# Neighbourhood-attention layer on one core: q and k of 14 heads computed first, as seven half-block products, through DRAM

## The chip, the core and the metric

The kernel runs on one core of a Trainium2 chip. The core has TensorE (PE, with its weight loads shown apart as PEld), VectorE (DVE), ScalarE (ACT), GpSimd (POOL) and SyncE (SP), which only starts transfers here; POOL starts transfers too. Each engine runs its instructions in the order in which they were written and waits for the others through semaphores. The metric is the time of one execution on the device, in microseconds (us).

## The reference, cut to what matters

All data is float32; the model width is 2048, there are 512 latent tokens (8 rows of 64), 256 context tokens and 16 heads of 128.

```python
h  = modulate(x,   sh1,  sc1)                  # 512 x 2048
hc = modulate(ctx, csh1, csc1)                 # 256 x 2048
q, k, v  = split(h @ w_qkv)                    # 16 heads of 128
k_c, v_c = split(hc @ w_qkv[:, 2048:])         # the context gives k and v alone
s_win = q_blk . k_blk * scale + bias           # 4 column bands of 128 queries; a band sees 2 or 3 key blocks of 128
s_ctx = q_blk . k_c * scale
p = softmax(concat([s_win, s_ctx]))            # one softmax over 256 or 384 window keys and 256 context keys
y = (p_win @ v_blk + p_ctx @ v_c) @ w_o
x = layer_norm(alpha * x + g1 * y)
x = layer_norm(alpha * x + g2 * swiglu(modulate(x, sh2, sc2)))
```

The shifts, scales and gates come from `silu(c) @ ada_w` (and from `c_ctx` for hc).

## The kernel before, in words

Each float32 operand of a large product is held as two parts, hi and lo, and each product is three matmuls (`mm3`): hi*hi, hi*lo, lo*hi. Weights come as raw tiles of 128x1024 (512 KB) on SP's queue; `pieces` (through `split`, L77 and L78) makes hi on ACT and lo on DVE. All matmuls are written by L81.

1. **Start phase.** For each of 16 slices of the width, `ada_start` streams four raw tiles `wr_an` through PE to get the modulation, `h_start` modulates a slice of x and of ctx and splits them into `a_h` and `hc`, and `qkv_start` accumulates q, k, v of heads 0 and 1 in seven banks `acc` (raw tiles `wr_w`). At its end the banks are split straight into the tiles that attention reads.
2. **Seven periods, one for each further pair of heads** (`hp` = 1 to 7). `v_block` makes v of both heads for the 6 token blocks (288 matmuls of 256 columns, banks `vp`). Then for each head `q_block` (48 matmuls of 512 columns, banks `qp`) and `k_block` (48 of 512 columns, `kp`, and 48 of 256 columns for the context, `cp`). Between them stand `ada_tile`s: two raw tiles `wr_ada` and two DVE multiply-and-sum instructions each (L141), which give the shifts, scales and gates that later stages need; 9 in each period, 64 in all.
3. **Attention.** `attn` cuts a head into 11 steps: four `score(j)` (matmuls into `sc` and `sl`, two maxima and a negation on DVE, two exponentials on ACT, the sum, its reciprocal and the scaling of p, L305, on DVE), then seven steps that transpose p, split it into `th` and `tl` and multiply by v into `o`. `enqueue` puts the steps in a list and `pop`, called between groups of matmuls, takes one now and then: head 2hp beside `k_block` of the next head (16 places), head 2hp+1 beside the next `v_block` (24 places). The result `ob` of a head goes to `oT` in DRAM on POOL's queue. DVE, ACT and POOL run what is written in that same order.
4. **Output projection** (`o_load`, `wo_half`), with attention of the last head beside it, and the remaining output blocks, LayerNorm, the feed-forward part and its LayerNorm. These products are `Pair`s run by `run`: a 2x2 arrangement of half blocks computed with seven half products in place of eight (24 matmuls of 256 columns each), with sums of weight halves on DVE (L623) and results put together from three banks (`post`).

A pool's tiles come free when their last reader is done, and a new pool that takes the place of an old one waits for all that used the old. `rp[0]` names the pool of raw tiles: `p0` with 6 buffers in the start phase, `p1r` with 3 in the periods. The lines that the change and the steps of the prediction touch: L77, L78, L141, L208 (load of x), L295 to L305 (softmax), L318 (transposes), L343 (`oT` write).

```python
            turn["mm"] = 0
            enqueue(attn(0, q0, k0, v0), 16)
            v_block(0, v0, [4, 5])
            for hp in range(1, NH // 2):
                if hp == 1:
                    enqueue(attn(1, q1, k1, v0), 24)
                v = new_v(hp)
                v_block(hp, v, list(range(6)))
                flush()
```

Of the kernel before, what the change touches and what calls it, by code (L numbers as in the profile page):

```python
# [17 lines left out]
P = 128  # L18
# [19 lines left out]
RAWBUFS = {"wraw": None, "r11": 2, "r22": 2, "r21": 1, "r12": 1}  # L38

# [4 lines left out]
def build(tc, ins, out):  # L44
    nc = tc.nc
    with ExitStack() as top:
# [60 lines left out]

        cv = base.tile([P, 2, KT], F32, name="cv")
# [43 lines left out]
        hcx = [cu_tile(k, F32R, f"hc{k}") for k in range(KT // 2)]  # L152
        hc_hi = [hcx[k // 2][:, k % 2 * T:k % 2 * T + C] for k in range(KT)]
        hc_lo = [hcx[k // 2][:, k % 2 * T + C:k % 2 * T + T] for k in range(KT)]

        with ExitStack() as ph1:
            pa = ph1.enter_context(tc.tile_pool(name="pa", bufs=1))

            def stage(name):
                return pa.tile([P, T], F32, tag="stg", name=name, bufs=2)  # L160

            def new_q(h):
                return [pa.tile([P, T], F32R, tag=f"q{i}", name=f"q{h}_{i}", bufs=2) for i in "hl"]

            def new_k(h):
                return [pa.tile([P, T + C], F32R, tag=f"k{i}", name=f"k{h}_{i}", bufs=2) for i in "hl"]

            def new_v(hp):
                return [[pa.tile([P, 2 * P], F32R, tag=f"v{t}{i}", name=f"v{hp}_{t}{i}") for i in "hl"]
                        for t in range(6)]  # L170

            def evac_q(ps, q):
                nc.scalar.activation(q[0], ps, AF.Copy, scale=QSCALE)
                nc.vector.scalar_tensor_tensor(out=q[1], in0=ps, scalar=QSCALE, in1=q[0].bitcast(F32),
                                               op0=ALU.mult, op1=ALU.subtract)

            q0, q1, k0, k1, v0 = new_q(0), new_q(1), new_k(0), new_k(1), new_v(0)
# [3 lines left out]

            accs = [bank(i, f"acc{i}") for i in range(7)]
            rows, mods = {}, {}
# [21 lines left out]
            def h_start(kt):  # L205
                md = mods.pop(kt)
                xr = stage(f"xr{kt}")
# [4 lines left out]
                cr = stage(f"cr{kt}")  # L212
                nc.gpsimd.dma_start(cr[:, :C], ins["ctxT"][kt])
# [4 lines left out]
            def qkv_start(kt):  # L218
                wh, wl = unit(ins["w0"][kt], f"w0{kt}", 768)
                f, l = kt == 0, kt == KT - 1  # L220
                for i in range(4):
                    sl = slice(i * P, (i + 1) * P)
                    mm3(accs[i], wh[:, sl], wl[:, sl], act_hi[kt], act_lo[kt], f, l)
                if kt + 1 < KT:
                    ada_cols(kt + 1)
# [940 lines left out]
```

## Time and profile before

| | us |
|---|---|
| median of 3 runs | 2516.32 |
| lowest and highest run | 2513.05, 2521.82 |
| the profiled execution, its own time | 2523.26 |
| its span in the trace | 2521.5 |
| busy in the span: PE, DVE, ACT, POOL | 2431.2, 1836.2, 1039.7, 232.1 |

Busy time is the time in which an engine runs instructions other than register, branch, semaphore and transfer-starting ones, so a busy PE can still be one whose matmuls follow each other more slowly than they could. The profiled execution lies 6.9 us above the median, and the sum below is made against it: from the span's start to 155.4 us is the start phase, from there to 945.3 us lie the first attention, the periods and the beginning of the output projection, whose first matmul starts there.

### The profile page before, as it was taken

To read this page: it belongs to the slowest core of one execution; us is meant where nothing else is said; L and a number is where in the kernel's file an instruction comes from. 1 tells how busy PE (TensorE), PEld (TensorE's weight loads), DVE (VectorE), ACT (ScalarE), POOL (GpSimd) and SP (SyncE) were. 2 spreads that over 40 slices of the span, in tenths; PEclk is the share of its full clock that TensorE was granted. 3 is DMA by queue.
4 is the path that set the end of the run, shared out by engine and by line. 5 is a ranking of instruction groups with operands and counts; after the bars stand their busy time and mean duration, and the time that the engine had idled before them with its cause. 6 is when DMAs were issued, how large, how long until landed. Compare 5 with 4: busy or idle time off the path is not lost.

```text
span 2521.5 us, 45143 instructions
## 1 busy us (share of the span) xinstructions
PE 2431.2 (96%) x18588; PEld 2303.4 (91%) x18588; DVE 1836.2 (73%) x2619; ACT 1039.7 (41%) x1590; POOL 232.1 (9%) x348
## 2 busy tenths in 40 slices
PE   7999999999999999999999999999999989999997
PEld 5688989888898988999999999999999989999996
DVE  2365655566565568899888888878888877878877
ACT  2242322222232235548444444444444544545555
POOL 1110100000010000110110100101001000000020
PEclk9999999999999999999999999999999999999998
DMA  8874444454455463745443434434344565755684
GB/s 328 317 246 151 153 162 134 153 163 151 155 156 163 128 202 130 191 100 187 136 136 118 136 124 138 137 120 133 125 144 156 182 186 134 210 146 134 175 185 118
DMA packets 142543, 406.18 MB, mean 161 GB/s; under 512 B 16544, under 2 KB 40496, under 8 KB 142208
## 3 DMA queue, kind: packets, MB, share of 16 engines
q1 hardware_dynamic: 116608, 342.42, 41.2%
q0 software_dynamic: 25728, 60.88, 9.9%
q8 instruction: 145, 2.38, 0.4%
q14 instruction: 62, 0.51, 0.1%
HBM read 351.85 MB, written 40.89 MB: 156 GB/s over the span
## 4 chain that ended last, share of the span: by engine, by line
issue 38%; PE 34%; DMA 11%; DVE 9%; POOL 4%; ACT 2%; SPq 0%; POOLq 0%; DVEq 0%; ACTq 0%
DMA wr_ada<-ada_t 7%; PE qp L81 6%; PE kp L81 4%; PE vp L81 3%; PE cp L81 2%; PE g_1b L81 2%; POOL setT L594 2%; DVE wr_ada L141 2%; PE y L81 2%; PE g_3b L81 1%; PE g_5b L81 1%; PE g_4b L81 1%; PE g_2b L81 1%; PE g_0b L81 1%; POOL setB L594 1%
## 5 line engine op out<-in xcount | busy, mean ns | idle before, releaser
L623 DVE TENSOR_TENSOR wr_f<-wr_f,wr_f 128x1024 f32<-128x1024 f32 x164 | 199.7, 1218 | 3.1 <-DMA wr_f<-w_in 1.7
L81 PE MATMUL vp<-wh_v,a_h 128*128 128x256 f32 x896 | 167.7, 279 | 0.0
L141 DVE CUSTOM_DVE_ANT_0 wr_ada<-wr_ada,s_c,bin 128x1024 f32<-128x1024 f32 x64 | 84.2, 1316 | 89.2 <-DMA wr_ada<-ada_t 88.9
L81 PEld LDWEIGHTS vp<-wh_v,a_h 128*128 128x128 f32 x896 | 141.2, 188 | 0.6
L81 PE MATMUL kp<-a_h,wh_k 128*128 128x512 f32 x448 | 141.2, 396 | 0.0
L81 PE MATMUL qp<-a_h,wh_q 128*128 128x512 f32 x448 | 140.6, 395 | 0.0
L141 DVE CUSTOM_DVE_ANT_0 wr_ada<-wr_ada,s_c,adap 128x1024 f32<-128x1024 f32 x64 | 82.2, 1284 | 79.3 <-DMA wr_ada<-ada_t 79.1
L81 PE MATMUL vp<-wl_v,a_h 128*128 128x256 f32 x448 | 125.1, 279 | 0.0
L623 DVE TENSOR_TENSOR wr_g<-wr_g,wr_g 128x896 f32<-128x896 f32 (+1 forms) x96 | 107.6, 1130 | 6.5 <-DMA wr_g<-w_out 5.5
L77 ACT CAST th<-tr 128x256 fp32r<-128x256 f32 (+2 forms) x96 | 45.8, 477 | 155.0 <-PE tr L318 154.9
L81 PEld LDWEIGHTS cp<-hc,wh_k 128*128 128x128 f32 x448 | 84.1, 188 | 20.3
L594 POOL DMA_DIRECT2D setB<-h x66 | 35.6, 542 | 711.1 <-DVE h L1008 692.6
L81 PE MATMUL vp<-wh_v,hc 128*128 128x256 f32 x512 | 98.3, 280 | 0.0
L81 PEld LDWEIGHTS qp<-a_h,wh_q 128*128 128x128 f32 x448 | 82.0, 188 | 16.5
L81 PE MATMUL cp<-hc,wh_k 128*128 128x256 f32 x448 | 89.5, 281 | 0.0
L301 ACT ACTIVATE p<-sc,sm 128x256 f32<-128x256 f32 x64 | 30.4, 475 | 143.2 <-DVE sm L299 143.2
L81 PE MATMUL qp<-a_h,wl_q 128*128 128x512 f32 x224 | 88.6, 395 | 0.0
L81 PE MATMUL kp<-a_h,wl_k 128*128 128x512 f32 x224 | 88.4, 395 | 0.0
L78 DVE TENSOR_TENSOR tl<-tr,th 128x256 fp32r<-128x256 f32 (+2 forms) x96 | 52.4, 552 | 48.0 <-ACT th L77 48.0
L81 PEld LDWEIGHTS vp<-wl_v,a_h 128*128 128x128 f32 x448 | 84.2, 188 | 0.6
L81 PEld LDWEIGHTS vp<-wh_v,hc 128*128 128x128 f32 x512 | 81.6, 188 | 0.1
L274 POOL TENSOR_TENSOR bv<-br,mask 128x256 f32<-128x256 f32 (+1 forms) x48 | 43.3, 928 | 399.9 <-DVE sm L304 370.3
(1882 smaller groups left out, 8516.1 us busy)
## 6 DMA issues: line engine op xcount, KB each, us to landing
wr_f<-w_in SPq DMA_DIRECT2D x164, 512.0 KB, 4.1
wr_ada<-ada_t SPq DMA_DIRECT2D x128, 512.0 KB, 3.9
wr_an<-ada_n SPq DMA_DIRECT2D x64, 512.0 KB, 7.4
wr_g<-w_out SPq DMA_DIRECT2D x64, 448.0 KB, 4.5
wr_v<-w_v SPq DMA_DIRECT2D x32, 512.0 KB, 4.6
wr_g<-w_out SPq DMA_DIRECT2D x32, 512.0 KB, 4.3
wr_q<-w_qk SPq DMA_DIRECT2D x28, 512.0 KB, 4.6
wr_k<-w_qk SPq DMA_DIRECT2D x28, 512.0 KB, 3.7
```

What stands on the lines that cost most here:

```text
L77: nc.scalar.copy(hi, src)
L78: nc.vector.tensor_tensor(out=lo, in0=src, in1=hi.bitcast(F32), op=ALU.subtract)
L81: nc.tensor.matmul(ps, a, b, start=start, stop=stop, skip_group_check=True)
L141: nc.vector.tensor_tensor_reduce(out=raw, in0=raw, in1=s_c[:, half * U:(half + 1) * U], scale=1.0, scalar=bin2[:, i:i + 1] if half == 0 el ...
L274: nc.gpsimd.tensor_tensor(out=bv[:, off:off + n * P].rearrange("p (d r k) -> p d r k", d=n, r=8), in0=brv[:, d0:d0 + n], in1=mask[:, off:o ...
L301: nc.scalar.activation(p[:, nl:nl + C], sc[:, :C], AF.Exp, bias=sm[:, 2:3], accum_out=sm[:, 3:4])
L594: nc.gpsimd.dma_start(setD[n][q], src)
L623: nc.vector.tensor_tensor(out=self.r[out][:, :n], in0=self.r[a][:, :n], in1=self.r[b][:, :n], op=op)
```

## The change

- **Start phase.** The slices come in the order 0, 8, 1, 9, ... The split `hc` tiles go to DRAM (`hcD`, 16 writes of 256 KB on POOL's queue). `h_sums` builds, from the x tiles of slices k and k+8, the four sums of activation halves that the seven half products need (`T1` to `T4`: 4 sums and 4 splits of 256 columns for each of 8 pairs of slices). At the end the seven banks `acc` are copied (ACT and DVE in turn) to tiles `st` and written to DRAM (`qkD`, `v0D`, `kc0D`).
- **A new stage** of 14 `QKPair`s (q and k of seven head pairs; 168 matmuls of 256 columns each), whose results go to `qkD` in DRAM. Beside them 14 `ada_tile`s.
- **Then** `hc` is loaded back (8 loads of 512 KB on SP's queue), and `v_block(0)` runs alone. A period is now `v_block` with attention of *both* heads of the pair before (22 steps at 24 places) and 7 ada tiles, then for each head a load of q and k from `qkD` (`qk_load`, POOL's queue, through the two `stg` buffers) and the context half of `k_block`. Attention of the last two heads, not of one, stands beside the output projection.
- **p is scaled on ACT**, not on DVE.
- `Pair` and `run` are moved up unchanged, but for the pool of their result tiles.

```diff
                     nc.vector.reciprocal(sm[:, 6:7], sm[:, 5:6])
-                    nc.vector.tensor_scalar_mul(p, p, sm[:, 6:7])
+                    nc.scalar.activation(p, p, AF.Identity, scale=sm[:, 6:7])
                     st[j] = (p, nl)
...
+                hcs[kt] = pa.tile([P, 2, C], F32R, tag="hcs", name=f"hcs{kt}", bufs=2)
+                split(hcs[kt][:, 0], hcs[kt][:, 1], cr)
+                nc.gpsimd.dma_start(hcD[kt], hcs[kt].bitcast(F32))
...
+            def h_sums(kk):
+                a, b = xs.pop(kk), xs.pop(kk + 8)
+                z = (a[:, HA], a[:, HB], b[:, HA], b[:, HB])
+                for n, d, x, y, op in (("T3", 1, 3, 1, ALU.subtract), ("T2", 0, 1, 0, ALU.add),
+                                       ("T4", 2, 2, 0, ALU.subtract), ("T1", 3, 3, 0, ALU.subtract)):
+                    nc.vector.tensor_tensor(out=z[d], in0=z[x], in1=z[y], op=op)
+                    split(sets[n](kk, 0), sets[n](kk, 1), z[d])
...
+                for i, dst in enumerate((qkD[0][0], qkD[1][0], qkD[0][1], qkD[1][1], v0D[0], v0D[1], kc0D)):
+                    st = p0.tile([P, T], F32, tag="xs", name=f"st{i}", bufs=4)
+                    if i % 2:
+                        nc.vector.tensor_copy(st, accs[i])
+                    else:
+                        nc.scalar.copy(st, accs[i])
+                    nc.gpsimd.dma_start(dst, st)
+            class QKPair(Pair):
...
+                    elif p == "P2":
+                        ada_more(1)
...
+            with tc.tile_pool(name="p1x", bufs=2) as p1x:
+                rp[0] = p1x
+                ev[0] = p1x
...
+                run([QKPair(w, j) for j in range(1, NH // 2) for w in range(2)], {})
...
+                    ada_more((2, 2, 2, 1)[u] if len(tl) > 2 else 0)
+                flush()
...
-            def q_block(h, q):
...
+            def qk_load(h):
+                q, k = new_q(h), new_k(h)
+                for w in range(2):
+                    st = stage(f"qk{w}_{h}")
+                    nc.gpsimd.dma_start(st, qkD[w][h])
...
-                        mm3(kb, hi[:, s_], lo[:, s_], act_hi[kt], act_lo[kt], kt == 0, kt == KT - 1)
                         mm3(cb[:, :C], hi[:, s_], lo[:, s_], hc_hi[kt], hc_lo[kt], kt == 0, kt == KT - 1)
...
             for hp in range(1, NH // 2):
-                if hp == 1:
-                    enqueue(attn(1, q1, k1, v0), 24)
+                enqueue(attn(2 * hp - 2, *qk[0], v) + attn(2 * hp - 1, *qk[1], v), 24)
                 v = new_v(hp)
                 v_block(hp, v, list(range(6)))
-                flush()
-                ada_more(3)
-                for i in range(2):
-                    h = hp * 2 + i
-                    q, k = new_q(h), new_k(h)
-                    q_block(h, q)
-                    ada_more(1)
-                    k_block(h, k)
-                    ada_more(2)
-                    flush()
-                    enqueue(attn(h, q, k, v), 16 if i == 0 else 24)
+                qk = []
+                for h in (2 * hp, 2 * hp + 1):
+                    qk.append(qk_load(h))
+                    k_block(h, qk[-1][1])
...
-            rate[0] = 12 / 21
+            enqueue(attn(NH - 2, *qk[0], v) + attn(NH - 1, *qk[1], v), 21)
```

Three places show how the instructions now stand. First, SP's queue where the start phase ends: `wr_w07` and `wr_w015` are the last weights of the start phase, `wr_v0_...` those of the first v block, `wr_qk0_1_...` those of the first new pair, and a row's brackets name the semaphores for which it waits. Before:

```order
81 L105 DMA wr_w015_1339<-w0 128x768 [waits DMAHW2_49,DVE_49]
82 L105 DMA wr_v0_0_1408<-w_v 128x1024
83 L105 DMA wr_v0_1_1462<-w_v 128x1024
84 L105 DMA wr_v0_2_1510<-w_v 128x1024 [waits DMAHW3_49]
```

Changed:

```order
80 L110 DMA wr_w07_1393<-w0 128x768 [waits DMAHW1_49,PE_49]
81 L110 DMA wr_w015_1445<-w0 128x768 [waits DMAHW2_49,DVE_49]
82 L153 DMA wr_qk0_1_11_1520<-w_qk 128x1024 [waits DMASW6_49,DMASW5_49,DMASW7_49,DMASW4_49,DMAHW0_49,DMASW3_49,DMAHW3_49,DMASW2_49,DMAHW4_49,DMASW1_49,DMAHW5_49,DMASW0_49,DMAHW6_49,DVE_49,DMAHW7_49,Activation_49,Pool_49]
83 L153 DMA wr_qk0_1_22_1522<-w_qk 128x1024
84 L153 DMA wr_qk0_1_21_1524<-w_qk 128x1024
```

The first load after the start phase waited for nothing; now it waits for ACT, DVE, POOL and for transfers of both queues, and POOL's queue stands as follows (`st` are the copies of the seven banks):

```order
61 L343 DMA hcD<-hcs_1271 128x512
62 L343 DMA hcD<-hcs_1362 128x512
63 L343 DMA hcD<-hcs_1441 128x512
64 L394 DMA qkD<-st_1493 128x512
65 L394 DMA qkD<-st_1499 128x512
66 L394 DMA qkD<-st_1496 128x512
67 L394 DMA qkD<-st_1502 128x512
68 L394 DMA v0D<-st_1505 128x512
69 L394 DMA v0D<-st_1508 128x512
70 L394 DMA kc0D<-st_1511 128x512
71 L421 DMA qkD<-yqk_1_1700 128x2x512
```

Seven writes now stand at the end of the start phase, where before there was none. Third, DVE where scores are made. Before (head 4, beside `k_block` of head 5; `sm` holds maxima and sums, the ISA rows are the add-and-max of a score or an ada tile's sum):

```order
376 L295 TENSOR_REDUCE sm4_1_3512<-sc4_1_3504 128x1
377 L296 ISA p4_1_3511,sm4_1_3512<-sl4_1_3503,bv4_3475 128x384
378 L296 ISA sm4_1_3512 128x1
379 L303 TENSOR_TENSOR sm4_0_3488<-sm4_0_3488 128x1
380 L141 ISA wr_ada_17_0_3794,adap17_3793<-wr_ada_17_0_3794,s_c_1402,bin2_88 128x1024
381 L141 ISA adap17_3793 128x1
382 L304 RECIPROCAL sm4_0_3488<-sm4_0_3488 128x1
383 L299 TENSOR_SCALAR sm4_1_3512<-sm4_1_3512 128x1
384 L305 TENSOR_SCALAR p4_0_3487<-p4_0_3487,sm4_0_3488 128x512
385 L78 TENSOR_TENSOR wl_k5_1_3704<-wr_k5_1_3701,wh_k5_1_3703 128x1024
```

Changed (head 6, beside `v_block` of the pair 8 and 9):

```order
788 L83 TENSOR_TENSOR wl_v4_1_7603<-wr_v4_1_7600,wh_v4_1_7602 128x1024
789 L501 TENSOR_SCALAR sm6_0_7468<-sm6_0_7468 128x1
790 L268 ISA wr_ada_37_0_7742,adap37_7741<-wr_ada_37_0_7742,s_c_97,bin2_88 128x1024
791 L268 ISA adap37_7741 128x1
792 L505 TENSOR_TENSOR sm6_0_7468<-sm6_0_7468 128x1
793 L497 TENSOR_REDUCE sm6_1_7498<-sc6_1_7490 128x1
794 L506 RECIPROCAL sm6_0_7468<-sm6_0_7468 128x1
795 L498 ISA p6_1_7497,sm6_1_7498<-sl6_1_7489,bv6_7455 128x384
796 L498 ISA sm6_1_7498 128x1
797 L268 ISA wr_ada_37_1_7745,ada_69<-wr_ada_37_1_7745,s_c_97,adap37_7741 128x1024
798 L268 ISA ada_69 128x1
799 L501 TENSOR_SCALAR sm6_1_7498<-sm6_1_7498 128x1
```

The scaling rows (L305) are gone from DVE, and an ada tile's sum (or a weight split, `wl_v4_1`) now stands in each score between the maximum and the negation (L501) that its exponentials wait for.

## Rows read from the trace of the kernel before

**Rows 1.** The page, busy time of the engines over the span.
```profile
PE 2431.2 (96%) x18588; PEld 2303.4 (91%) x18588; DVE 1836.2 (73%) x2619; ACT 1039.7 (41%) x1590; POOL 232.1 (9%) x348
```

**Rows 2.** Stretches: length, PE, PEld, DVE, ACT, POOL busy, PE clock, DMA share, GB/s.
```profile
0.00:155.00 155.00, 132.64 (x1054) 97.71 (x1055) 54.82 (x111) 40.17 (x73) 20.41 (x45) 0.97 0.90 325
...
223.30:332.70 109.40, 107.19 (x697) 97.34 (x697) 64.29 (x129) 31.09 (x69) 7.69 (x10) 1.00 0.48 153
...
770.40:879.70 109.30, 107.35 (x697) 97.39 (x696) 64.11 (x131) 31.09 (x69) 7.69 (x10) 1.00 0.48 153
...
1950.00:2000.00 50.00, 50.00 (x427) 50.00 (x426) 39.57 (x45) 20.60 (x25) 3.95 (x8) 1.00 0.53 176
```

**Rows 3.** The chain that ended last: start, us, what (x instructions).
```profile
150.27 5.16 PE acc L81 x30
155.43 2.42 PE vp L81 x21
...
162.01 2.80 PE vp L81 x24
...
332.73 11.20 PE qp L81 x48
...
1067.54 19.77 PE y5b L81 x168
```

**Rows 4.** Transfers in 60 to 130 us, GB/s in 40 slices.
```profile
GB/s 309 328 389 376 373 82 73 239 293 407 419 316 307 368 383 400 200 265 337 411 422 215 311 325 405 407 237 260 337 382 403 154 157 304 405 406 399 215 269 372
```

**Rows 5.** Groups in 223.3 to 332.7 us: count | busy, mean ns | idle before them, releaser.
```profile
L141 DVE CUSTOM_DVE_ANT_0 wr_ada<-wr_ada,s_c,bin 128x1024 f32<-128x1024 f32 x9 | 11.9, 1327 | 10.9 <-DMA wr_ada<-ada_t 10.8
...
L78 DVE TENSOR_TENSOR wl_q<-wr_q,wh_q 128x1024 fp32r<-128x1024 f32 x4 | 4.9, 1222 | 9.5 <-ACT wh_q L77 9.5
...
L301 ACT ACTIVATE p<-sc,sm 128x256 f32<-128x256 f32 x8 | 3.8, 475 | 19.1 <-DVE sm L299 19.1
L305 DVE TENSOR_SCALAR p<-p,sm 128x640 f32<-128x640 f32 x4 | 3.7, 917 | 0.0
...
L295 DVE TENSOR_REDUCE sm<-sc 128x1 f32<-128x256 f32 x8 | 3.4, 420 | 0.1
...
L302 ACT ACTIVATE p<-p,sm 128x384 f32<-128x384 f32 x4 | 2.4, 607 | 0.0
...
L299 DVE TENSOR_SCALAR sm<-sm 128x1 f32<-128x1 f32 x8 | 1.7, 210 | 0.1
...
L305 DVE TENSOR_SCALAR p<-p,sm 128x512 f32<-128x512 f32 x4 | 2.2, 548 | 0.1
L296 DVE CUSTOM_DVE_ANT_0 p<-sl,bv 128x384 f32<-128x384 f32 x4 | 2.2, 546 | 0.1
```

**Rows 6.** Waits of PE in 223.3 to 879.7 us: total, times, longest.
```profile
PE o L81 <- DVE tl L78: 9.8, 7, 1.8
PE tr L318 <- DVE sm L296: 2.6, 4, 1.0
```

**Rows 7.** Transfers by name over the span: count, KB each, us from issue to landing.
```profile
wr_v<-w_v SPq DMA_DIRECT2D x32, 512.0 KB, 4.6
...
oT<-ob POOLq DMA_DIRECT2D x15, 256.0 KB, 3.2
```

**Rows 8.** The start phase by ACT and POOL, 128x512 pieces: count | busy, mean ns | idle.
```profile
L77 ACT CAST a_h<-xr 128x512 fp32r<-128x512 f32 x16 | 9.9, 620 | 68.8 <-DVE xr L209 68.8
...
L208 POOL DMA_DIRECT2D xr<-xT x16 | 8.7, 542 | 123.6 <-DVE a_h L78 123.6
```

**Rows 9.** Stretches in a later change of stage, columns as in rows 2.
```profile
2025.20:2030.60 5.40, 0.06 (x1) 0.00 (x0) 5.40 (x10) 0.42 (x1) 1.55 (x3) 0.63 0.37 107
2030.60:2036.80 6.20, 6.18 (x29) 6.18 (x30) 5.55 (x8) 1.05 (x1) 1.67 (x4) 0.50 0.93 329
```

**Rows 10.** The chain in that change of stage, columns as in rows 3.
```profile
2038.52 1.05 ACT T_p L77
...
2039.60 1.24 DVE T_p L78
```

More of the change, by code (lines that the diff above doesn't have):

```diff
@@ L106, in unit, with k256, __init__, __call__ @@
             return pieces(raw, name, n)
+        def k256(ap):
+            return ap.rearrange("p (k t) -> p k t", t=HT)
+        class Cuts:
+            def __init__(self, cuts):
+                self.cuts = cuts
+            def __call__(self, k, i):
+                for k0, k1, t in self.cuts:
+                    if k < k1:
+                        return t[:, k - k0, i]
+            def fill(self, a, b, src):
+                for k0, k1, t in self.cuts:
+                    lo, hi = max(a, k0), min(b, k1)
+                    if lo < hi:
+                        split(t[:, lo - k0:hi - k0, 0], t[:, lo - k0:hi - k0, 1], src[:, lo - a:hi - a])
@@ new lines, in run, with prep @@
+        def run(items_of, ends, mid=None, fill=None):
+            items = [(i, p) for i in range(len(items_of)) for p in items_of[i].order]
+            def prep(x):
+                if x < len(items):
+                    i, p = items[x]
+                    if fill:
+                        fill(i, p)
+                    items_of[i].prep(p)
+            items_of[0].load()
+            prep(0)
+            prep(1)
+            if mid:
+                mid()
+            for x, (i, p) in enumerate(items):
+                if p == "P4" and i + 1 < len(items_of):
+                    items_of[i + 1].load()
+                if i in ends:
+                    if p == ORDER[0]:
+                        zload = ends[i].load()
+                        for _ in range(3):
+                            next(zload)
+                    else:
+                        next(zload, None)
+                prep(x + 2)
+                items_of[i].mul(p)
+                items_of[i].post(p)
+                if i in ends:
+                    ends[i].after(p)
@@ L182, in build @@
+            for n in ("T2", "T1"):
+                sets[n] = Cuts([(0, 8, pt.tile([P, 8, 2, HT], F32R, name=f"{n}h"))])
             accs = [bank(i, f"acc{i}") for i in range(7)]
-            rows, mods = {}, {}
+            rows, mods, xs, hcs = {}, {}, {}, {}
             def ada_start(kt):
@@ new lines, in build @@
+            with tc.tile_pool(name="p1x", bufs=2) as p1x:
+                rp[0] = p1x
+                ev[0] = p1x
+                nc.gpsimd.dma_start(s_c, ins["c"].partition_broadcast(P))
+                nc.scalar.activation(s_c, s_c, AF.Silu)
+                sets.update({"B11": quarter(0, HA), "B21": quarter(1, HA), "B22": quarter(1, HB)})
+                turn["all"] = 7
+                run([QKPair(w, j) for j in range(1, NH // 2) for w in range(2)], {})
+            pts.close()
+            hcx = [cu_tile(k, F32R, f"hc{k}") for k in range(KT // 2)]
@@ new lines, in stage, with new_q, new_k, new_v @@
+            def stage(name):
+                return pa.tile([P, T], F32, tag="stg", name=name, bufs=2)
+            def new_q(h):
+                return [pa.tile([P, T], F32R, tag=f"q{i}", name=f"q{h}_{i}", bufs=2) for i in "hl"]
+            def new_k(h):
+                return [pa.tile([P, T + C], F32R, tag=f"k{i}", name=f"k{h}_{i}", bufs=2) for i in "hl"]
+            def new_v(hp):
+                return [[pa.tile([P, 2 * P], F32R, tag=f"v{t}{i}", name=f"v{hp}_{t}{i}") for i in "hl"]
+                        for t in range(6)]
```

352 lines of the change are left out of this document (169 added, 183 removed).

## The prediction

> **What bounds the kernel now.** The page comes first: TensorE is busy for 96% of the span, VectorE for 73%, ScalarE for 41% [rows 1]. That is an average, so I read the stretches that the change touches, one by one. In the start phase the transfer engines are busy for 0.90 of the time and move 325 GB/s, while PE is busy for 132.64 of 155 us [rows 2]: transfers and PE limit each other there. Every period lasts 109.4 us at a granted clock of 1.00, with PE busy for 107.2 us but DVE for only 64.3 and ACT for 31.1 [rows 2]; the first and the last of the seven are shown. So the periods belong to PE. The chain of waits gives PE's prices. In 162.01 us 24 matmuls of 256 columns follow each other in 2.80 us, 0.117 us each; 48 of 512 columns take 11.20 us, 0.233 each; and a block of seven half products, 168 matmuls, takes 19.77 us [rows 3]. From these I count what PE has to do in a period: v 288 x 0.117 = 33.7, q and k of two heads 4 x 11.2 = 44.8, context k 2 x 48 x 0.117 = 11.2, sum 89.7. Attention of a head has 24 matmuls of 256 columns, 12 of 384, 6 of 512 and 18 transposes of 128; by columns that is 24 x 0.117 + 12 x 0.175 + 6 x 0.233 + 18 x 0.06 to 0.07 = 7.6 us, 15.2 for two. Together 104.9, so 4.5 us of a period's 109.4 are lost. Part of it is seen as waits of PE for the split of transposed p (9.8 us over six periods) and for scores (2.6) [rows 6].
>
> **What is saved on PE.** q and k of two heads cost 44.8 us now and two seven-product blocks, 2 x 19.77 = 39.5 us, afterwards. Over seven pairs that is 36.8 us less. It is the only large gain; every other term is a place where the saving can be lost. The stretch from 155.4 to 945.3 us lasts 789.9 us; I build its successor.
>
> **Start phase.** Sixteen writes of 256 KB are added, 4.2 MB. If the transfers bind, they cost 4.2 MB at 325 GB/s = 13 us [rows 2]. If the tenth of idle transfer time takes them in, 0: slices of 2 us reach 422 GB/s where others fall to 73 [rows 4], so there are holes, but the holes come where loads wait for buffers. I take the middle, +7. The sums of x halves (per two slices 4 sums and 4 splits on DVE and 4 casts on ACT) cost nothing: DVE is busy for 54.8 and ACT for 40.2 of 155 us [rows 2]; without that cover their 8 x 12 instructions of some 0.3 to 0.4 us would cost up to 35 us.
>
> **The entry to the new stage.** Before, the first v block's loads waited for nothing and PE went from the last `acc` matmul (150.27 + 5.16) to `vp` at 155.43 without a gap [rows 3]. Now the new pool stands where `p0` stood, so the first pair's weights wait for the last of seven bank copies to land in DRAM. Copies of the last bank: 0.62 us; the write's issue: 0.54 [rows 8]; its landing: 3.2; then a weight load, 4.6 [rows 7]; its cast and its low part, 1.05 and 1.24 [rows 10]. End to end that is 11.3 us; with some issue and copy time beside the last matmuls I take 10.5 (8 to 13). After such a gap the clock is low: in a later change of stage PE idled for 5.36 of 5.40 us, and the next 6.20 us ran at a granted clock of 0.50 (1.2 GHz), 29 matmuls in 6.2 us where 0.117 x 29 = 3.4 would do [rows 9]. So +2.8 us. Together **13.3**.
>
> **The new stage.** 14 x 19.77 = 276.8 us. Ada tiles stand beside the first seven pairs, two a pair. In the feed-forward part DVE is busy for 39.57 of 50 us [rows 2], 15.6 us a pair; four ada sums of 1.33 [rows 5] bring it to 20.9 at most, less where a pair here has no gating product to make, against PE's 19.8. So DVE is about level with PE. The price lies between 0 (19 us of DVE work fit) and 20 us for all seven (transfers late as well); I take **+3**.
>
> **The entry to the periods.** `wr_v0_0` waits for the last matmul of the last pair, since `hc` and the raw tiles take over memory from the sets of sums: load 4.6 and cast 1.05, about 5.5 us without PE, and 2.8 us of low clock as above: **8.3**. `v_block(0)` then runs alone, 96 x 0.117 = **11.3** us (before, it had attention of head 0 between its matmuls). Meanwhile v, q, k and the context k of heads 0 and 1 come back by seven loads of 256 KB on POOL's queue, behind the last pair's write and the mask, through two buffers. Four rounds of 3.2 us landing [rows 7] plus 0.62 for the copy out [rows 8] and about as much on DVE are some 18 us, behind a write that lands first. The scores of head 0 wait for these: **+10** (0 to 14).
>
> **A period.** PE's work falls to 33.7 + 11.2 + 15.2 = 60.1 us. DVE keeps most of its own: 64.3 less 5.9 for the scaling of p (eight instructions), 4.9 for the low parts of q's weights, 5.2 for four of 18 ada sums [rows 5] is 48.3 us. Neither is full, but the cover is thinner: 22 attention steps stand at 24 places of one v block, where 11 stood at 24, so a step has about 12 v matmuls (1.4 us) behind it. Score j+2 can start only when the exponential of score j has read its bank, and that waits for reduction, add-and-max and negation on DVE in order. In the order of the changed kernel one ada sum or weight split (1.22 to 1.33 us) stands inside this chain. 0.42 + 0.55 + 0.21 + 1.3 on DVE and 0.475 on ACT [rows 5] are about 3.2 us with the hand-overs, against 3.7 us of PE work between a score and the next but one. One foreign instruction fits, two do not. Ends: 60.1 (nothing is lost) and 73 (each of eight scores loses one more foreign instruction, 1.0 us net, on top of today's loss: 64.7 + 8.3). With today's loss alone a period takes 60.1 + 4.6 = 64.7; I take **67**, as in the written order three scores in eight have two foreign instructions in front. Seven are 469 us.
>
> The three raw buffers turn round 22 loads in a period. One turn is 4.6 us of landing [rows 7], 1.3 us of use and some waiting, 6.5 us; 22 x 6.5 / 3 = 48 us, not last. ACT gains eight scalings; exponentials of 384 columns take 0.61 [rows 5], so I allow 0.8 for 640 columns. ACT, at 31 us of a period before, has room, so I set nothing for it in the sum; but the transposes wait for it 0.3 us longer than for DVE's 0.55 [rows 5] (its 0.917 mean holds two slow ones). At worst 8 x 0.3 x 7 = 17 us. The Trainium skill, ScalarE: Activation LUTs, Rules for kernel authors, says to do a multiplication on VectorE and not on ScalarE, and budgets about 0.3 us and 0.83 ns an element, an estimated 0.83 us for 640 elements; this speaks against the last part of the change, and by it the time would be 2555 us, 17 more than mine. DVE's row agrees that DVE is faster alone; but DVE is the fuller engine.
>
> **Output projection.** Attention of head 14 moves here, 7.6 us, and the end of two heads' attention behind fewer matmuls: **+5** (0 to 10).
>
> **The sum.** 13.3 + 276.8 + 3 + 8.3 + 11.3 + 10 + 469 + 12.6 = 804.3 against 789.9, and 7 in the start phase: +21.4 us. The profiled execution would go from 2523.26 to 2544.7; against the median of the runs, 2516.3, which is 6.9 us lower, **2538 us**.
>
> **The rivals.** *Faster.* Everything that can be hidden is hidden: start phase 0, entry 8 + 2.8, no loss from ada tiles, entry to the periods 4 + 2.8 + 11.3 + 3, periods at 64.7 (452.9), output projection 7.6. 769.2 against 789.9: -20.7, 2496 us. For it: DVE falls below three quarters of a period, and in the feed-forward part DVE at 39.57 of 50 us costs PE nothing, PE 50.00 [rows 2]. Against it: five separate covers have to hold, and the entry gaps are visible in the written order. *No change that can be measured.* Periods lose no more than today, 64.7, and the rest is as forecast: 21.4 - 16.1 = +5, 2522. *Slower by more.* DVE's written order decides each score, 73 us a period: 21.4 + 42 = +63, 2580 us. It decides once two foreign instructions stand in front of most negations. For it: today's exponentials already wait 19.1 us a period for the negation [rows 5]; then PE had q and k blocks to run meanwhile, which are gone.
>
> **How the numbers follow.** Forecast, between +8 and +45 us: 0.42. Faster rival, anything below -7.5: 0.24. No measurable change: 0.18. Slower rival: 0.16. A measurement of this kernel can tell about 0.3% from no change, 7.5 us. So faster 0.24, same 0.18, slower 0.58. The range reaches from the faster rival's 2496 to the slower one's 2580; the part outside is half of each rival. The likeliest case's own range is 2524 to 2561.
>
> **What would show it.** Right: a PE gap of about 10 us after the last `acc` matmul and about 5 after the last pair, each with a granted clock of 0.50 behind it; pairs of about 20 us; 65 to 70 us from one context k block to the next, with PE's waits in the v block named `sc` or `sl` behind ACT's exponentials. Wrong: pairs well above 20 us in the first seven and 19.8 in the last seven (DVE bound by ada sums), periods at or above 72 us or at 62 and below, or a start phase longer by 13 us or more.

## The result and the profile after

The changed kernel takes 2583.26 us (median of 4 runs, 2576.92 to 2588.69) against 2515.22 us for the kernel before in the same comparison: a ratio of 1.0265, interval 1.0234 to 1.0296. It is slower by 68 us. The forecast was 2538 with a range from 2496 to 2580; the sign was right, the size was not, and the time lies outside the range. Its slower rival had 2580.

The page of the changed kernel's profiled execution, busy time of the engines, against [rows 1]:

```profile
PE 2423.7 (94%) x19596; PEld 2339.4 (90%) x19596; DVE 1993.0 (77%) x2804; ACT 1179.0 (46%) x1788; POOL 283.9 (11%) x420
```

PE is busy for 7.5 us less in a span that is 65.4 us longer (2586.9 against 2521.5): what was saved on matmuls is lost in waits, and in matmuls that run slowly. Where, the stretches tell. The columns are those of [rows 2]: length, PE, PEld, DVE, ACT, POOL busy, PE clock, DMA share, GB/s.

```profile
0.00:156.70 156.70, 128.62 (x1056) 94.47 (x1056) 72.96 (x171) 48.60 (x102) 30.61 (x65) 1.00 0.90 333
156.70:168.20 11.50, 0.00 (x0) 0.00 (x0) 0.69 (x1) 1.63 (x2) 1.63 (x3) 0.72 0.67 224
168.20:174.00 5.80, 5.28 (x30) 4.99 (x31) 5.04 (x5) 2.50 (x4) 0.00 (x0) 0.67 1.00 397
174.00:339.60 165.60, 161.38 (x1318) 157.52 (x1317) 147.90 (x173) 61.29 (x71) 5.01 (x7) 1.00 0.63 211
339.60:459.20 119.60, 119.60 (x1009) 119.39 (x1007) 85.73 (x87) 45.37 (x52) 4.28 (x6) 1.00 0.42 141
459.20:464.70 5.50, 0.00 (x0) 0.00 (x0) 1.81 (x3) 1.04 (x1) 0.72 (x1) 0.77 0.77 232
...
566.70:639.00 72.30, 64.67 (x507) 61.84 (x506) 50.06 (x111) 32.84 (x72) 11.27 (x14) 1.00 0.58 185
```

Row by row: the start phase ends at 156.7 (before: 155.4). Then PE has nothing for 11.5 us, and 5.8 us at a granted clock of 0.67. Eight pairs with ada tiles beside them end at 339.6, six without at 459.2: 21.4 and 19.9 us a pair. A gap of 5.5 us follows. The last row is one period, from the end of one pair of context k blocks to the next; the six of that kind end at 999.7, so one takes (999.7 - 566.7) / 6 = 72.2 us. The first one, with `v_block(0)` in front, lasts from 464.7 to 566.7, 102 us.

What PE waits for from the last pair to the output projection (459 to 1003 us; total, times, longest), against [rows 6]:

```profile
PE sc L86 <- ACT p L503: 23.4, 14, 2.5
PE o L86 <- DVE tl L83: 14.5, 17, 2.7
```

The waits for `sc` are new. Before, no score waited for an exponential; now 14 waits do so, all of them in the six periods.

### The profile page after: what moved, and what is told of

The parts are those of the page before. It is cut to its first block, busy times and chain, and to the rows that moved or that the text cites. A ratio compares the mean times of both kernels' runs of the same rounds, so it can differ in the third digit from the quotient of the medians.

```text
span 2586.9 us, 48038 instructions
## 1 busy us (share of the span) xinstructions
PE 2423.7 (94%) x19596; PEld 2339.4 (90%) x19596; DVE 1993.0 (77%) x2804; ACT 1179.0 (46%) x1788; POOL 283.9 (11%) x420
## 4 chain that ended last, share of the span: by engine, by line
PE 50%; DMA 16%; issue 15%; DVE 12%; ACT 4%; POOL 2%; SPq 0%; POOLq 0%; ACTq 0%; DVEq 0%
DMA wr_ada<-ada_t 4%; PE f L86 2%; DMA qk<-qkD 2%; PE vp L86 2%; DMA wr_v<-w_v 2%; PE g_1b L86 2%; DVE wr_ada L268 2%; PE qk_7b L86 2%; PE qk_5b L86 2%; PE qk_6b L86 2%; DMA wr_k<-w_qk 1%; PE g_4b L86 1%; PE g_5b L86 1%; PE g_3b L86 1%; PE g_2b L86 1%
## 5 line engine op out<-in xcount | busy, mean ns | idle before, releaser
L86 PE MATMUL vp<-wh_v,a_h 128*128 128x256 f32 x896 | 180.9, 285 | 1.5 <-ACT wh_v L82 1.5
L157 DVE TENSOR_TENSOR wr_g<-wr_g,wr_g 128x896 f32<-128x896 f32 (+1 forms) x96 | 107.5, 1129 | 5.6 <-DMA wr_g<-w_out 4.6
L268 DVE CUSTOM_DVE_ANT_0 wr_ada<-wr_ada,s_c,adap 128x1024 f32<-128x1024 f32 x64 | 82.4, 1288 | 23.5 <-DMA wr_ada<-ada_t 23.4
L86 PE MATMUL cp<-hc,wh_k 128*128 128x256 f32 x448 | 79.8, 281 | 0.0
L476 POOL TENSOR_TENSOR bv<-br,mask 128x256 f32<-128x256 f32 (+1 forms) x48 | 54.1, 1154 | 202.1 <-DVE sm L498 195.5
L86 PE MATMUL vp<-wl_v,hc 128*128 128x256 f32 x256 | 74.2, 290 | 0.7 <-DVE wl_v L83 0.7
L157 DVE TENSOR_TENSOR wr_qk<-wr_qk,wr_qk 128x1024 f32<-128x1024 f32 x56 | 67.8, 1219 | 3.5 <-DMA wr_qk<-w_qk 3.0
L86 PEld LDWEIGHTS cp<-hc,wh_k 128*128 128x128 f32 x448 | 68.7, 188 | 0.0
L86 PE MATMUL cp<-hc,wl_k 128*128 128x256 f32 x224 | 62.9, 281 | 0.0
L507 ACT ACTIVATE p<-p,sm 128x512 f32<-128x512 f32 (+1 forms) x64 | 49.2, 773 | 21.8 <-DVE sm L506 17.9
L520 PE MATMUL tr<-ident,p 128*128 128x128 f32 x288 | 50.5, 275 | 4.3 <-DVE sm L498 3.2
L83 DVE TENSOR_TENSOR wl_k<-wr_k,wh_k 128x1024 fp32r<-128x1024 f32 x28 | 34.3, 1224 | 26.2 <-ACT wh_k L82 26.2
```

The costliest lines, as they stand in the source:

```text
L83: nc.vector.tensor_tensor(out=lo, in0=src, in1=hi.bitcast(F32), op=ALU.subtract)
L86: nc.tensor.matmul(ps, a, b, start=start, stop=stop, skip_group_check=True)
L157: nc.vector.tensor_tensor(out=self.r[out][:, :n], in0=self.r[a][:, :n], in1=self.r[b][:, :n], op=op)
L268: nc.vector.tensor_tensor_reduce(out=raw, in0=raw, in1=s_c[:, half * U:(half + 1) * U], scale=1.0, scalar=bin2[:, i:i + 1] if half == 0 el ...
L476: nc.gpsimd.tensor_tensor(out=bv[:, off:off + n * P].rearrange("p (d r k) -> p d r k", d=n, r=8), in0=brv[:, d0:d0 + n], in1=mask[:, off:o ...
L507: nc.scalar.activation(p, p, AF.Identity, scale=sm[:, 6:7])
```

## The experiments

Lengths of periods are taken as above, from the end of a period's context k blocks to the next, mean of six. The table puts the outcome ahead.

| kernel | us (median) | period, us |
|---|---|---|
| before | 2515 to 2519 | 109.5 |
| changed | 2583 | 72.2 |
| x1: no ada tiles beside v blocks | 2536.2 | 64.9 |
| x2: their sums without their loads | 2536.1 | 65.3 |
| x3: p scaled on DVE | 2567.4 | 69.1 |
| x4: weights of v and k in buffers of their own | 2585.1 | 70.2 (three of 75.5, three of 64.8) |
| x5: five raw buffers | 2589.3 | 72.8 |
| y1: sums tied to attention steps | 2551.0 | 66.5 |
| y2: y1 with p scaled on DVE | 2565.2 | 68.6 |
| y3: y2, tied beside the pairs too | 2559.0 | 68.4 |
| w3: a third buffer for q and k, alone | 2571.5 (one run) | 70.1 |
| w4: y1 with the third buffer | 2541.0 | 65.0 |
| w1: w4, pairs tied, entry shortened | 2524.9 | 64.7 |
| w2: w1, first v block written first | 2522.9 | 64.9 |
| z1: before, p scaled on ACT | 2528.7 | 110.2 |
| z2: before, sums tied | 2512.9 | 108.0 |
| z3: before, sums tied, p scaled on ACT | 2512.9 | 107.5 |

### Do ada tiles cost it, and which part of them: x1, x2

x1 leaves the tiles out (a constant stands for what they give); x2 keeps the sums where they stand and takes the loads away, so they sum other data.

```diff
+        nc.gpsimd.memset(ada, 0.25)
...
-                    ada_more((2, 2, 2, 1)[u] if len(tl) > 2 else 0)
```

```diff
-                nc.sync.dma_start(raw, ins["ada_t"][i, :, half * U:(half + 1) * U])
+                if i < 14:
+                    nc.sync.dma_start(raw, ins["ada_t"][i, :, half * U:(half + 1) * U])
                 nc.vector.tensor_tensor_reduce(
-                    out=raw, in0=raw, in1=s_c[:, half * U:(half + 1) * U], scale=1.0,
+                    out=raw, in0=raw if i < 14 else s_c[:, (1 - half) * U:(2 - half) * U], in1=s_c[:, half * U:(half + 1) * U], scale=1.0,
```

> Leaves out the 49 ada tiles beside the v blocks (their shifts, scales and gates are a constant instead). The changed kernel takes 72.2 us from the end of one period's context k blocks to the next. Theory A (ada tiles stand in the way of attention, by their DVE sums or by their loads): 62 to 64 us a period, 55 to 70 us off the whole. Theory B (22 attention steps at 24 places are too dense by themselves, scores wait for banks): 69 us or more. Theory C (q and k come back from DRAM too late at each period's end): 69 us or more, with the waits at the first scores of a period.

> Keeps all DVE sums of ada tiles 14 to 63 in their places, but takes their loads away (they sum a resident tile, so those shifts, scales and gates are other numbers). If the loads or the three raw buffers are what ada tiles cost (theory A1): 62 to 66 us a period, near the kernel without them. If the sums in DVE's written order cost it (theory A2): 70 to 72 us a period, as in the changed kernel.

One period of x1, columns as above:

```profile
558.90:623.40 64.50, 63.31 (x506) 61.41 (x505) 33.88 (x83) 32.14 (x73) 9.30 (x14) 1.00 0.30 97
```

And of x2:

```profile
555.90:621.20 65.30, 63.70 (x507) 61.59 (x506) 50.66 (x111) 32.73 (x72) 11.28 (x14) 1.00 0.31 96
```

DVE has 16.8 us more to do in x2 than in x1 and the period is 0.8 us longer in these rows, 0.4 in the mean. In the written order half of the 48 scores of heads 2 to 13 have one foreign instruction between the first maximum and the negation, and none has two, in the changed kernel and in x2 alike. So what the sums and their order cost by themselves is about 0.4 us a period, and 6.9 us of 72.2 go with the loads. Without ada tiles a period is close to the 64.7 us that today's loss would give. The gain of x1 is a little under what theory A had expected (64.9 us a period against 62 to 64, 47 us off the whole against 55 to 70); theories B and C had 69 or more.

### Is it the buffers: x4, x5

```diff
-        def unit(src, name, n=U):
-            raw = raw_tile(name)
+        def unit(src, name, n=U, tag=None):
+            raw = raw_tile(name, tag)
...
-                    hi, lo = unit(ins["w_v"][hp, :, u * U:(u + 1) * U], f"v{hp}_{u}")
+                    hi, lo = unit(ins["w_v"][hp, :, u * U:(u + 1) * U], f"v{hp}_{u}", tag="wv")
```

```diff
-            rp[0] = ph1.enter_context(tc.tile_pool(name="p1r", bufs=3))
+            rp[0] = ph1.enter_context(tc.tile_pool(name="p1r", bufs=5))
```

> Weights of v and k in the periods get two raw buffers of their own beside the three, so that a v weight no longer stands behind ada loads that wait for buffers. Theory A1 (raw buffers): 66 to 69 us a period, 25 to 40 us off the whole. Theories A2, B, C: within 1 us of 72.2.

> Five raw buffers in the periods in place of three, nothing else. Shown so far: ada tiles cost 7 us a period by their loads, not by their sums. Theory L (DVE reaches a sum before its load has landed and the scores behind it wait; more buffers let the load start earlier): 66 to 69 us a period. Theory M (the order of sums follows the buffers, so the sums move forward as far as the loads do): about 72 again, or periods of unlike length.

Neither helps. In x4 the ada tiles ran ahead: periods of 75.5, 76.6 and 74.4 us with their loads, then 64.7, 65.2 and 64.6 with none left, 2585 in all; neither theory had expected that. The first three periods hold 71 half sums there, against 42 in the changed kernel. More room moves the sums forward as far as the loads, and DVE meets them no later. DVE's waits for these loads from 566 to 930 us, five periods (total, times, longest), in the changed kernel:

```profile
DVE wr_ada L268 <- DMA wr_ada<-ada_t: 28.9, 21, 3.3
```

In x5:

```profile
DVE wr_ada L268 <- DMA wr_ada<-ada_t: 41.2, 28, 2.8
```

DVE stands still for 5.8 us a period in the first, for 8.2 in the second.

### Is it the wait in written order, or the traffic: y1

y1 keeps all loads and sums. A tiny DVE instruction in front of each half's sum reads a result of the attention step beside it, so the sum comes behind that step in DVE's order; loads of ada have three buffers, the weights two of their own (as x4).

```diff
+                nc.vector.scalar_tensor_tensor(out=tied, in0=late, scalar=0.0, in1=start,
+                                               op0=ALU.mult, op1=ALU.add)
...
+                    late[0] = sm[:, 2:3]
                     nc.scalar.activation(p[:, nl:nl + C], sc[:, :C], AF.Exp, bias=sm[:, 2:3], accum_out=sm[:, 3:4])
...
                         pop()
-                    ada_more((2, 2, 2, 1)[u] if len(tl) > 2 else 0)
+                        places += 1
+                        if late[0] is not None and done < min(14, places * 14 // 22):
+                            done += 1
+                            ada_late(late[0])
```

> Each half of an ada tile's sum is tied by a tiny DVE instruction to a result of the attention step beside it (the negated maximum, or the low part of a transposed block), so that it cannot stand in front of that step, and its load has three buffers of its own; weights of v and k have two. Sums and loads are all there. If DVE's wait for a load in written order is the cost (theory L): 65 to 67 us a period, as without loads, and DVE's waits for ada tiles under 2 us a period. If the loads cost by their traffic (theory T, 190 GB/s beside the weights): 71 us or more.

Its second period, columns as above:

```profile
627.60:693.90 66.30, 64.16 (x507) 62.13 (x506) 53.39 (x124) 32.29 (x72) 10.13 (x14) 1.00 0.64 203
```

66.5 us in the mean, and the list of waits has no DVE wait for an ada load left, though the transfers are denser than in the changed kernel (0.64 and 203 GB/s against 0.58 and 185). So it is not the traffic: it is DVE standing in front of a load with the work of attention queued behind. y1 also has the buffers of x4; these alone did not help, and the tie without them was not run.

The trace of the changed kernel shows three kinds of such places (start, us, engine, line, instruction, and in brackets the wait before it and what ended it). In the first, DVE waits for the load of an ada tile, and the low part of a transposed block stands behind it:

```profile
809.59 1.28 DVE L268 CUSTOM_DVE_ANT_0 wr_ada<-wr_ada,s_c,bin 128x1024 f32<-128x1024 f32 x1 [3.25 <-DMA wr_ada<-ada_t]
...
810.80 1.28 DVE L83 TENSOR_TENSOR tl<-tr,th 128x512 fp32r<-128x512 f32 x2
```

PE waits for that low part:

```profile
811.54 0.50 PE L86 MATMUL o<-tl,v_4h 128*128 128x512 f32 x1 [2.68 <-DVE tl L83]
```

In the second, ACT waits for a weight of k, DVE waits for ACT, and a score stands behind:

```profile
604.61 1.05 ACT L82 CAST wh_k<-wr_k 128x1024 fp32r<-128x1024 f32 x1 [6.80 <-DMA wr_k<-w_qk]
```

```profile
605.70 1.23 DVE L83 TENSOR_TENSOR wl_k<-wr_k,wh_k 128x1024 fp32r<-128x1024 f32 x1 [3.56 <-ACT wh_k L82]
606.84 0.42 DVE L497 TENSOR_REDUCE sm<-sc 128x1 f32<-128x256 f32 x1
```

```profile
608.50 0.39 PE L86 MATMUL sc<-k_h,q_h 128*128 128x256 f32 x1 [1.60 <-ACT p L503]
```

These weights go through the same three raw buffers as the ada tiles, and their loads wait on SP's queue for ada sums that free a buffer. Over the six periods (566.7 to 999.7 us) the waits of SP with a weight's load, and of DVE for the cast of a k weight, are:

```profile
SPq L110 <- DVE ada L268: 39.3, 18, 4.2
```

```profile
DVE wl_k L83 <- ACT wh_k L82: 24.3, 18, 3.9
```

Over the six periods of x2 the second of these is 3.5 us, of y1 2.3. In the third kind, DVE waits for k from DRAM, and an ada sum and a weight split stand before the negation:

```profile
643.27 0.69 DVE L83 TENSOR_TENSOR k_l<-qk,k_h 128x512 fp32r<-128x512 f32 x1 [1.16 <-ACT k_h L82]
...
644.22 1.27 DVE L268 CUSTOM_DVE_ANT_0 wr_ada<-wr_ada,s_c,adap 128x1024 f32<-128x1024 f32 x1
...
645.42 0.42 DVE L497 TENSOR_REDUCE sm<-sc 128x1 f32<-128x256 f32 x1
645.75 0.41 DVE L498 CUSTOM_DVE_ANT_0 p<-sl,bv 128x256 f32<-128x256 f32 x1
...
646.17 1.23 DVE L83 TENSOR_TENSOR wl_v<-wr_v,wh_v 128x1024 fp32r<-128x1024 f32 x1
647.32 0.21 DVE L501 TENSOR_SCALAR sm<-sm 128x1 f32<-128x1 f32 x1
```

ACT, whose exponential waits for that negation:

```profile
647.56 0.47 ACT L503 ACTIVATE p<-sc,sm 128x256 f32<-128x256 f32 x1 [1.42 <-DVE sm L501]
```

And PE, whose next score but one waits for the bank:

```profile
648.17 0.39 PE L86 MATMUL sc<-k_h,q_h 128*128 128x256 f32 x1 [2.00 <-ACT p L503]
```

Of the 14 waits for `sc`, nine (15.7 us) lie where v_block begins, behind a wait of the third kind, and five (7.7 us) behind one of the second; in none was DVE's last wait before them for the load of an ada tile. DVE's waits for ada loads mostly come before PE's waits for `tl` and for transposes instead. So the chain is the one that the prediction described, but what makes it long is DVE's late arrival, after a load, more than the foreign instruction inside; and the ada loads reach the scores through the buffers and the order, not by DVE's wait for them.

### Scaling p: x3, y2, z1, z3

```diff
-                    nc.scalar.activation(p, p, AF.Identity, scale=sm[:, 6:7])
+                    nc.vector.tensor_scalar_mul(p, p, sm[:, 6:7])
```

x3 does this to the changed kernel, y2 to y1. z1 does the reverse to the kernel before, z3 to z2 (below).

> Undoes one part: p is scaled on DVE again. If scaling on ScalarE costs latency, as its slower row says (0.77 against 0.55 us): 1 to 2 us less a period, 2570. If DVE is the fuller engine and its order decides: 2 to 4 us more a period, 2600 to 2610. No difference if neither stands in the chain.

> The same with p scaled on DVE. If ScalarE's longer scaling stands in the chain of a score also without the late loads: 1 to 2 us a period less than with it on ScalarE. If it only mattered behind late loads: the same, or 1 us more because DVE is fuller.

> The kernel before with one part of the change alone: p scaled on ScalarE. DVE loses 5.9 us of 64.3 in each period and ScalarE has 31 of 109 busy. If the scaling on DVE delays scores (theory: shorter DVE order): up to 2 us of the 4.5 lost in a period come back, 5 to 14 us off, 2503 to 2511. If the longer scaling of ScalarE delays the transposes: 0 to 10 us more.

The groups of this line over one period (count | busy, mean ns | idle), in the changed kernel:

```profile
L507 ACT ACTIVATE p<-p,sm 128x640 f32<-128x640 f32 x4 | 3.3, 825 | 0.0
L507 ACT ACTIVATE p<-p,sm 128x512 f32<-128x512 f32 x4 | 2.9, 722 | 1.6 <-DVE sm L506 1.6
```

In x3:

```profile
L507 DVE TENSOR_SCALAR p<-p,sm 128x640 f32<-128x640 f32 x4 | 3.3, 826 | 0.1
...
L507 DVE TENSOR_SCALAR p<-p,sm 128x512 f32<-128x512 f32 x4 | 2.0, 490 | 0.0
```

The signs differ by kernel. Scaling on DVE takes 3.1 us off a period of the changed kernel, adds 2.1 where sums are tied (more than either branch for y2 had); scaling on ACT adds 0.7 to a period of the kernel before (2528.7 us, ratio 1.005, interval 1.0033 to 1.0067) and takes 0.5 off where it has tied sums, with no difference in the whole time (2512.9 us both). Where DVE's order is free, the waits for loads go with it: DVE's waits for ada loads over the same five periods are 28.9 us in the changed kernel (above), and in x3:

```profile
DVE wr_ada L268 <- DMA wr_ada<-ada_t: 14.9, 11, 2.4
```

So in the changed kernel this part of the change costs some 16 us, and half of DVE's waits for loads come with it; where the order of its sums is held it is a gain. That these waits are the whole of the 16 us was not shown.

The four runs also limit what the tie is worth. With p scaled on ACT it takes 5.7 us off a period, with p on DVE only 0.5 (x3 69.1, y2 68.6; 2567.4 and 2565.2 us), although no wait for an ada load is left there either. From x3 to y2 PE's waits for `sc` fall from 16.3 to 5.8 us over the six periods, but those for `tl` rise from 6.9 to 13.1 and those of transposes for DVE from 1.0 to 6.4. So how much is lost with these loads depends on what else DVE has to do.

### The pairs: y3

```diff
                         Pair.post(self, p)
-                    elif p == "P2":
-                        ada_more(1)
+                        ada_late(self.v[:, 0:1])
...
                         nc.scalar.copy(self.y[:, 0], b0[:, HA])
+                        ada_late(self.y[:, 3, 0:1])
```

> The same, and beside the pairs of q and k each half of an ada tile is tied to a result of its pair, one tile a pair for all 14 in place of two a pair for the first eight. The first eight pairs took 21.4 us each, the last six 19.9. If DVE is over full with two tiles: all pairs 19.8 to 20.0, 10 us off the stage. If the pairs are slow for another cause (late weights): 21 us as before.

The stage falls from 290.9 to 283.2 us; after the first (23.3 us, it holds the low clock) every pair takes 20.0. In the changed kernel DVE is busy for 147.9 of the 165.6 us of its early pairs (above), and its waits there are:

```profile
DVE wr_ada L268 <- DMA wr_ada<-ada_t: 14.3, 7, 3.3
```

147.9 + 14.3 = 162.2 of 165.6: DVE is the bound there, two tiles a pair and their loads together.

### q and k from DRAM, and the entries: w3, w4, w1, w2

```diff
-                return pa.tile([P, T], F32, tag="stg", name=name, bufs=2)
+                return pa.tile([P, T], F32, tag="stg", name=name, bufs=3)
```

w1 also puts the seven bank copies into weight tiles, so that the first pair's load no longer waits for them to land:

```diff
-                    st = p0.tile([P, T], F32, tag="xs", name=f"st{i}", bufs=4)
+                    if i % 2 == 0:
+                        st2 = wp.tile([P, U], F32R, tag=("whi", "wlo")[i // 2 % 2], name=f"st{i}")
+                    st = st2[:, i % 2 * T:i % 2 * T + T].bitcast(F32)
```

w2 moves `v_block(0, v, [4, 5])` ahead of the loads of q, k and v of heads 0 and 1, and the mask's load to the stage before.

> The changed kernel with three in place of two buffers for q and k from DRAM, nothing else. If these buffers cost a part of its own at each period's end: 70 to 71 us a period instead of 72.2. If they lie beside DVE's waits for ada loads: 72.

> Tied sums beside attention and the third buffer. If the third buffer made the difference between 66.5 and 64.7 us: 64.7 a period. If it came from the pairs or entries (ada tiles further along): 66.5.

> The changed kernel with tied sums beside attention and beside the pairs, p scaled on ScalarE, the seven bank copies in the weights' tiles so that the first pair's load no longer waits for them to land in DRAM, and a third buffer for q and k. From runs so far: 2551 with tied sums in the periods, 8 less from the pairs, 5 to 6 less at the entry of the new stage (its gap of 11.6 us falls to about 6): 2536 to 2540. If the entry's gap stays above 10 us the landing of the copies was not what held the load.

> The best kernel so far of the changed order (periods 64.7 us, 97 us from the last pair to the end of the first context k blocks), with the first v block written ahead of the loads of q, k and v of heads 0 and 1, and the mask loaded in the stage before. If ScalarE's wait for v of heads 0 and 1, in front of the casts of weights, and the late loads behind the mask are what is lost there: 5 to 10 us off, 2515 to 2520. If only the landing of the last pair's write counts: under 3 us.

The third buffer is worth 2.1 us a period in the changed kernel, where PE's waits for `sc` fall from 23.4 to 14.0 us over the six periods, and 1.4 with tied sums. At the entry the gap falls from 11.6 to 7.6 us, less than I expected: the landing of the copies had held the load, and now it starts at 158.0 us, where the last `acc` matmul ends, and takes 6.0 us to land. w1 comes out 11 to 15 us lower than the sum of the parts said, at 2524.9 us; the third buffer, which had not been counted, is worth 10 of it (w4 against y1). Against the kernel before w1 is 1.0025 (interval 1.0012 to 1.0037), so it is still no gain. w2 gains nothing where it was meant to: from the last pair to the end of the first context k blocks it takes 97.3 us, w1 96.9, and its ratio, 1.0021 (interval 1.0008 to 1.0033), can't be told from that of w1. Which of the waits there would have to go stays open.

### The kernel before with tied sums: z2, z3

The edit is that of y1, put behind the steps of a period's attention (18 halves), with the weights of q, k and v in two buffers of their own.

> The kernel before with its ada sums tied to attention steps (18 halves over the 20 steps of a period), loads of ada in three buffers and weights in two of their own; p scaled on DVE. If late ada loads in DVE's written order cost the kernel before too: 5 to 20 us off. If its 23 us of DVE waits for loads a period lie beside PE's q and k blocks and cost nothing: within 5 us of 2516, or more where sums now stand among scores.

> Both of these. If they add up: the sum of the two differences. In the changed kernel ScalarE's scaling was worth 2.1 us a period with tied sums and cost 3.1 with sums free to stand in front of scores; the same here would give 10 us off against the tied kernel with p scaled on DVE.

Both are a little faster than the kernel before: 0.9978 (interval 0.9963 to 0.9992) and 0.9976 (0.9962 to 0.9989). The waits of DVE for ada loads, 22.8 us in a period before, cost PE little there: with none left (z2) a period is 1.5 us shorter. PE had no wait during any of them in the period of [rows 5]; some 14 us of them lay beside q and k blocks, the others beside a v block with half as many attention steps as now. z3 was expected 10 us below z2 if the parts add up as in the changed kernel; it is level with it. These two are the only versions that beat the kernel before, by some 5 us.

## Why the prediction was wrong, step by step

| step | forecast, us | measured, us |
|---|---|---|
| start phase longer | 7 | 1.3 |
| gap at the entry of the new stage | 10.5 | 11.6 |
| pairs, with the low clock | 282.6 | 290.9 |
| gap at the entry of the periods | 5.5 | 5.5 |
| first v block and first period, with low clock and late loads | 91.1 | 102.0 |
| six periods | 402 | 433.0 |
| output projection, beyond before | 12.6 | 15.8 |

**Right.** What bounds the kernel before, the saving on PE (six pairs without ada tiles took 19.9 us each), both entry gaps and their causes, and, but for 3 us, the move of attention into the output projection. The chain at the entry reads as summed up (start, us, what):

```profile
160.32 2.31 DMA kc0D<-st
162.82 3.93 DMA wr_qk<-w_qk
```

**Wrong: the period at 67 us.** This step carries 31 of the 49 us by which the time to the end of the output projection's first blocks went beyond the forecast (1070.5 against 1000.3 us, 70 us later, where 21 was forecast). What follows there is unchanged code and took 1516.4 against 1521.2 us; this was not followed up. The direction was right, and the place too: scores wait for the exponential of the score but one before, behind DVE. But the prediction priced the foreign instructions inside that chain by their durations, 1.2 to 1.3 us, and set the wait of DVE for the loads at nothing, as three raw buffers turn round in 48 us. x2 shows the sums and their order to cost 0.4 us a period, and the loads 6.9; y1 shows that it is not their traffic: with DVE's waits for ada loads and for the k weights queued among them gone, 72.2 becomes 66.5. The first of [rows 5] had 10.8 us of DVE's waits for ada loads in a period of the kernel before, and the other half of the sums has 12.0 more, in the same columns:

```profile
L141 DVE CUSTOM_DVE_ANT_0 wr_ada<-wr_ada,s_c,adap 128x1024 f32<-128x1024 f32 x9 | 11.6, 1284 | 12.0 <-DMA wr_ada<-ada_t 12.0
```

The prediction says nothing of these 22.8 us. PE lost only 4.5 in a period and did not show them; the change takes away much of what lay beside them. The count of foreign instructions was wrong too: three scores in eight were said to have two in front of the negation, and in the section on the change each score has one. In the written order 24 of the 48 have one and none has two; in the kernel before 6 of the same 48 have one. And the slower rival, 73 us, had the right size by the wrong price, which was luck.

**Wrong: two stage buffers for q and k cost nothing in a period.** The prediction set them into the first period alone. w3 shows 2.1 us in every period.

**Wrong: the pairs at +3.** The bounds, 0 to 20, held; it is about 9 (the eight pairs took 171.4 us against 8 x 19.9, and 2.8 of the rest is the low clock as forecast). DVE was put level with PE, but the +3 left out the waits for loads, which only the upper bound had: 14.3 us of them.

**Undersized: the first period.** The waits are about as forecast, 12.4 us: 1.5 and 2.8 for weights, 5.7 and 2.4 for k. But the clock, low behind the entry's gap as forecast, fell again, and this was not in the sum. Stretches of the changed kernel, columns as above:

```profile
464.70:470.00 5.30, 4.60 (x23) 4.31 (x24) 2.60 (x3) 2.10 (x2) 0.00 (x0) 0.60 0.92 301
...
478.00:486.00 8.00, 3.76 (x20) 3.35 (x19) 6.69 (x9) 1.78 (x4) 6.20 (x6) 0.79 0.50 158
486.00:494.00 8.00, 2.67 (x13) 2.38 (x12) 0.26 (x1) 0.92 (x2) 0.00 (x0) 0.50 0.56 176
494.00:502.00 8.00, 6.92 (x31) 6.17 (x31) 6.53 (x13) 3.17 (x6) 1.62 (x3) 0.65 0.65 216
502.00:510.00 8.00, 5.79 (x26) 5.79 (x27) 5.93 (x16) 4.02 (x11) 0.00 (x0) 0.57 0.46 146
510.00:518.00 8.00, 8.00 (x70) 7.94 (x70) 7.89 (x18) 4.71 (x13) 4.99 (x4) 1.00 0.64 211
```

From 486 to 510 us the granted clock is 0.50 to 0.65; PE is busy for 15.4 us of it with 13 + 31 + 26 = 70 matmuls; the next 70 take 8.0 us at 1.00. So some 7 us go there.

**Oversized: the start phase.** +7 was taken between 0 and 13; it took 1.3 us more, at 333 in place of 325 GB/s. That is 52.2 MB in place of 50.4, so of the 4.2 MB added only 1.8 came on top: the first loads of v weights, which before fell at the end of this stretch, are gone from it, and the prediction did not count that. Whether the holes would have taken in all 4.2 is not shown.

A slip without weight: by [rows 9] PE idled for 5.34 of 5.40 us, not 5.36.

**Weighed and half right: the scaling.** The Trainium skill, ScalarE: Activation LUTs, Rules for kernel authors, says to multiply on VectorE. For 512 elements the rows agree, 0.722 against 0.490 us. The run that undoes the scaling gains 16 us, close to the 17 that I allowed at worst, but not by that price: with the order of the sums held in the changed kernel, ScalarE is the better place (y1 against y2, 14 us).

## What to carry to other kernels

An engine that runs in written order turns every load it waits for into a wait of all that is queued behind it; before work is taken from the bottleneck, look at which waits of the other engines lie under that work, since they can come out when it goes. Loads that share buffers share the wait, so a late side load also makes the urgent loads behind it late. A consumer of a load that nothing urgent needs belongs behind the urgent instructions, by a tie if the order can't be written; more buffers alone moved the wait forward. And a saving on matmuls that adds stages has to pay for each stage's entry: here some 12 and 6 us of idle PE, with a granted clock of 0.67 and 0.60 in the stretches behind.

## What the runs showed of the hardware

The granted clock has two levels, 0.50 and 1.00 (1.2 and 2.4 GHz); a value between them is the mean of a stretch. In the changed kernel it did not only fall in the long gaps of PE at the entries (11.5 and 5.5 us). It also fell in the first period, in waits of PE of 2.8 and 2.4 us, and was then still at 0.51 over 5.8 us in which PE was busy throughout. Stretches, columns as above:

```profile
480.70:483.30 2.60, 0.00 (x0) 0.00 (x0) 2.60 (x4) 0.00 (x0) 2.60 (x2) 0.87 0.27 63
501.90:504.10 2.20, 0.00 (x0) 0.00 (x0) 2.20 (x5) 0.35 (x2) 0.00 (x0) 0.77 0.44 119
504.20:510.00 5.80, 5.79 (x26) 5.79 (x27) 3.77 (x11) 3.57 (x10) 0.00 (x0) 0.51 0.46 154
```

In the period shown above it stays at 1.00, but in three of the six it falls for 3.4 us, in or just behind a wait for `sc` of 2.0 to 2.6 us; the first of them:

```profile
793.30:796.60 3.30, 3.30 (x16) 3.30 (x15) 3.30 (x12) 1.73 (x5) 0.00 (x0) 0.50 0.84 273
```

Waits of much the same length elsewhere left it at 1.00, as that of 2.68 us at 811.54.

Scaling 128x512 takes 0.722 us on ScalarE and 0.490 on VectorE over one period; 128x640 takes 0.825 and 0.826 in the mean, where VectorE's mean holds slow ones (over the whole of x3 its scalings take 0.470 to 1.286 us, ScalarE's in the changed kernel 0.706 to 0.832).
